# Low parts of branch weights made by VectorE a step earlier, twelve more blocks per layer moved from accumulating DMA to VectorE, and the vector transposes asked for later

## The chip, the cores and the metric

The kernel runs on one core of one Trainium2 chip. The metric is the device time of one execution, in microseconds (us). "Before" is the kernel without the change, "after" the kernel with it.

## What is computed

The reference is a two-layer encoder over two sequences of 256 positions, 1024 channels wide, in float32. Each layer normalises its input, multiplies it by one wide matrix, feeds five branches from the columns of the product (differential attention, a short gated convolution, a Conformer convolution of 31 taps, latent attention, attention to a memory), multiplies each branch by its own 512x1024 matrix, mixes the five by sigmoid gates and projects the mixture once more:

```python
h = _rms_norm(x, norm_pre)
proj = h @ w_in
(a_q, a_k, a_v, a_z, b_b, b_c, b_x, b_z, c_glu, c_z,
 d_cq, d_ckv, d_kr, d_z, e_q, e_z, gates) = jnp.split(proj, split_idx, axis=-1)
...
u = _dwconv(glu_a * jax.nn.sigmoid(glu_b), conf_dw_w) + conf_dw_b
o_c = jax.nn.silu(_layer_norm(u, conf_ln_g, conf_ln_b))
...
g = jax.nn.sigmoid(gates.reshape(B, S, N_BRANCHES, D_MODEL))
y = g[:, :, 0] * (outs[0] @ w_branch[0])
for i in range(1, N_BRANCHES):
    y = y + g[:, :, i] * (outs[i] @ w_branch[i])
y = y @ w_out
return x + _rms_norm(y, norm_post)
```

## The kernel before

Both sequences together are 512 rows. **Each product is made of three**: an operand x is kept as a high part (x rounded to TensorE's shorter float32 form) and a low part (x minus the high part), and `mm3` (L128 to L131) multiplies high by high (L129), high by low (L130 or L131) and low by high into one PSUM bank. So every weight block, 128 partitions by up to 1024 columns, is loaded by the SP queue into a tile of the `f` pool (12 buffers) and then split.

**Splitting** is `split` (L298 to L328). The high part `wh` is always a copy by ScalarE (L134). The low part `wl` is made in one of two ways: by VectorE, which subtracts (L295), or, where the block is marked `by_dma`, by ScalarE writing the negated block into `wl` (L322) and a DMA on GpSimd's queue that adds the block to it there (L323). `wh` and `wl` come from rings of NSPLIT = 4 buffers each, so the fifth split waits until the matmuls of the first are through. Marked in before are per layer the 36 blocks of the steps `s_q`, `s_k`, `zE`, `s_v`, `s_d` (832 columns wide), `bsteps[0]` and `bsteps[1]`, and the 20 blocks `wb` of the branch matrices: 112 in all.

**The order of the work** is a list of steps. A full step is 24 matmuls of 512 columns. Per layer it runs through value, key and memory products, the Conformer's gate product (`cglu`), `s_q`, `s_k`, `zE`, `s_v`, `s_d`, `bsteps[0]`, two small steps of the latent attention, `bsteps[1]`, `zC`, `zA`, `zD`, then five gate branches and the output product. A gate branch is seven products of gates (the last are called S4 and X22; X22 reads the two blocks `V4`) and four `b_step`s, which multiply the branch by its blocks `wb` 0 to 3: two steps on `wb` 0 and 1, then two on `wb` 2 and 3. Attention, layer norms and the 31 taps of the convolution (L622, L626) are background work, `bg`, of which a piece is written out after each step. Taps are tied by `issue_after` to the last VectorE subtraction written out ahead of them.

**When a block is split** is set by `issue_splits` (L1233), called ahead of each step: it splits on to the fourth block counted from the step's own first. Two blocks `o` per branch (the branch's activations) have room of their own outside the rings but are counted here, too. At X22's step the four are `V4` 0 and 1 and `o` 0 and 1, so all four `wb` are split at the first `b_step`.

**At the start** the small parameter vectors are loaded into rows of one buffer, `vecs`. `setup_vectors` transposes them on TensorE (L203) into `chv` and makes the lambda of the differential attention; it is called ahead of the first step.

Of the kernel before, what the change touches and what calls it, by code (L numbers as in the profile page):

```python
# [41 lines left out]
NSPLIT = 4  # L42
# [36 lines left out]
def body(ctx, tc, xp, xs_, mp, ms, norm_pre, w_in, diff_lambda, diff_subln, sconv_w,  # L79
# [23 lines left out]
    def nm(s):  # L103
        uid[0] += 1
        return f"{s}_{uid[0]}"
# [7 lines left out]
    def f4(dt=F32):  # L113
        return wk.tile([128, D], dt, tag="f4", name=nm("f4"), bufs=12)

    def m2(dt=F32):
        return wk.tile([128, 512], dt, tag="m2", name=nm("m2"), bufs=10)
# [7 lines left out]
    def att(slot, shape=None, dt=F32):  # L125
        return big.tile(shape or [128, 4, 512], dt, tag=f"att{slot}", name=nm(f"att{slot}"))
# [54 lines left out]
        nc.gpsimd.dma_start(dl, diff_lambda.rearrange("l a d -> (l a d)").partition_broadcast(128))  # L181
        yield

    vecs = att(8)
    rowsm, rows1, rows5, dl = vecs[:, 0, 0:128], vecs[:, 1, 0:128], vecs[:, 2], vecs[:, 3]

    def setup_mem_gains():
        t1 = trb()
# [11 lines left out]
    def setup_vectors():  # L200
        t5 = trb()
        for m in range(4):
            nc.tensor.transpose(t5[:, m * NR5:(m + 1) * NR5], rows5[0:NR5, m * 128:(m + 1) * 128],  # L203
                                ident[0:NR5, 0:NR5])
        copy(chv, t5[:, 0:4 * NR5].rearrange("p (m r) -> p m r", m=4))
        d4 = dl.rearrange("p (l a b d) -> p l a b d", l=DEPTH, a=2, b=2)
        pr = m2()
        p4 = pr[:, 0:DEPTH * 128].rearrange("p (l a d) -> p l a d", l=DEPTH, a=2)
        for li in range(DEPTH):
            nc.vector.tensor_mul(p4[:, li], d4[:, li, :, 0], d4[:, li, :, 1])  # L210
        s4 = sm(4, "lam")
        nc.vector.tensor_reduce(s4, p4.rearrange("p l a d -> p (l a) d"), AX.X, ALU.add)
        e4 = sm(4, "lam")
        nc.scalar.activation(e4, s4, AF.Exp)
        e2 = e4.rearrange("p (l a) -> p l a", a=2)
        nc.vector.tensor_sub(nlam.rearrange("p (l o) -> p l o", o=1), e2[:, :, 1:2], e2[:, :, 0:1])
        for li in range(DEPTH):
            nc.vector.tensor_scalar(nlam[:, li:li + 1], nlam[:, li:li + 1], -LAM_INIT[li], None, ALU.add)
# [113 lines left out]
    bg = []  # L332
# [201 lines left out]
    def layer(li):  # L534
# [51 lines left out]
        s_q = b_steps(wi, OFF["a_q"], 512, hT, post_qk("qT", 0))  # L586
        s_k = b_steps(wi, OFF["a_k"], 512, hT, post_qk("kT", 1))
# [9 lines left out]
        s_v = b_steps(wi, OFF["a_v"], 512, hT, post_va)  # L597
# [115 lines left out]
        zE = z_out(4, OFF["e_z"], "oE", 4)  # L713
# [33 lines left out]
        bsteps = []  # L747
# [42 lines left out]
        s_d = b_steps(wi, OFF["d_c"], 416, hT, post_d)  # L790
# [63 lines left out]
                              for s in range(2) for h0 in (0, 2)], 2))  # L854
        s_mq, s_mkv = Step(pq, pe_mq, post_mq), Step(pkv, pe_mkv, post_mkv)

        for s_ in s_q + s_k + zE + s_v + s_d + bsteps[0] + bsteps[1]:
            for pc in s_.pieces:
                pc.raw.by_dma = True
        steps.extend(cglu + s_q + s_k + zE + s_v + s_d + bsteps[0] + [s_mq, s_mkv] + bsteps[1] + zC + zA + zD)  # L860
# [95 lines left out]
        def gate_branch(n):  # L956
            i, q = ORDER[n], qs4[n]
            nxt = early(qs4[n + 1]) if n + 1 < NB else None
            item = {}
# [40 lines left out]
                add("o", lambda j=j: ozt[j], j, L_(4 + j), dest=o_room(j))  # L1000
            for j in range(4):
                add("wb", (lambda j=j: wbt[j]), j, L_(6, 7) if j == 0 else [], after=A_(2 + j) if j < 2 else None)
                item["wb", j].by_dma = True

            def product(x, w, bank, first, last):

# [200 lines left out]
    raws = []  # L1207
    for s_ in steps:
        for pc in s_.pieces:
            if pc.raw not in raws:  # L1210
                raws.append(pc.raw)
        s_.base = min((raws.index(pc.raw) for pc in s_.pieces), default=len(raws))
    loads = []
    for raw in raws:
        loads.extend(raw.loads)
        raw.need = len(loads)
    nl, nsp = [0], [0]

    def issue_raws(most=1 << 30):
# [11 lines left out]
        issue_raws()  # L1231

    def issue_splits(s_):  # L1233
        while nsp[0] < min(len(raws), s_.base + NSPLIT):
            split_next()

    def run():
# [56 lines left out]
            some_consts(99)  # L1294
        st["memT"] = (hs, ls)
        setup_gains()
        setup_vectors()

        def first_x():
            hs = [big.tile([128, 4, 512], F32R, tag=f"hTh{g}", name=nm("hTh")) for g in range(2)]  # L1300
# [19 lines left out]
        bg_drain()  # L1320

    run()


# [42 lines left out]
```

## Time and profile before

| | |
|---|---|
| time, median of 3 runs | 1652.76 us (1647.35 to 1655.71) |
| the profiled execution | 1652.49 us, of which the span from first to last instruction is 1650.7 us |
| TensorE (PE) busy | 1608.2 us, 97% of the span |
| VectorE (DVE) | 1104.1 us, 67% |
| ScalarE (ACT) | 924.0 us, 56% |
| GpSimd (POOL) | 179.9 us, 11% |
| mean granted TensorE clock | 0.997 |

TensorE is busy nearly always, so what matters are the few stretches in which it stands still and the few in which its clock is granted at half. The profile names for every wait what ended it. A busy share is of the whole span; the stages differ, and one of them may have VectorE full while another leaves it idle.

### The profile page before, as it was taken

The page shows a single profiled execution, that of the slowest core. Times are in us where ns is not written, and L with a number is a line of the kernel's source. Part 1 is how long each engine was busy: PE and PEld are TensorE (multiplying, and loading weights), DVE is VectorE, ACT ScalarE, POOL GpSimd, SP SyncE. Part 2 cuts the span into 40 slices and gives each one's busy share as a digit, 9 for nine tenths or more (in the row PEclk, how much of TensorE's full clock was granted, in tenths as well). Part 3 has the DMA queues.
Part 4 walks back from the last instruction along what each step waited for, and adds up shares of the span by engine and source line. Part 5 has one row for each costly group of instructions (what it writes and reads, how often), then busy time and mean ns, then how long its engine had stood idle before and what let it go on. Part 6 is the DMA issues. An engine that isn't in the chain of part 4 may idle for free.

```text
span 1650.7 us, 20815 instructions
## 1 busy us (share of the span) xinstructions
PE 1608.2 (97%) x7658; PEld 1333.3 (81%) x7658; DVE 1104.1 (67%) x1788; ACT 924.0 (56%) x1562; POOL 179.9 (11%) x248
## 2 busy tenths in 40 slices
PE   6999999999999999999999999999999999999998
PEld 5888887778888888787888888877888877877886
DVE  5459935778884675674672799268779755865753
ACT  5446547798444744645453655577964545545542
POOL 3001122111000000001020011221100000000010
PEclk9999999999999999999999999999999999999999
DMA  8317866545536546546461297665455357357341
GB/s 284 101 37 190 209 157 137 128 115 153 172 122 178 153 131 175 159 135 167 151 188 30 71 231 176 142 139 131 115 162 185 117 142 204 107 159 196 103 115 51
DMA packets 137350, 240.25 MB, mean 146 GB/s; under 512 B 15455, under 2 KB 67717, under 8 KB 137248
## 3 DMA queue, kind: packets, MB, share of 16 engines
q1 hardware_dynamic: 114176, 159.40, 31.3%
q0 software_dynamic: 22464, 78.46, 22.0%
q8 instruction: 60, 0.98, 0.2%
q10 hardware_dynamic: 608, 1.06, 0.2%
q14 instruction: 42, 0.34, 0.1%
HBM read 166.27 MB, written 14.68 MB: 110 GB/s over the span
## 4 chain that ended last, share of the span: by engine, by line
PE 38%; issue 7%; DMA 3%; DVE 3%; ACT 2%; POOL 0%; POOLq 0%; DVEq 0%; ACTq 0%
PE acc L130 11%; PE acc L129 11%; PE acc L131 11%; DMA wl<-f 1%; DMA f<-in_w_in_dram 1%; DVE wl L295 1%; PE tr L431 1%; ACT wh L134 1%; PE tr L239 0%; ACT att L134 0%; PE tr L1088 0%; PE tr L513 0%; PE tr L129 0%; PE tr L131 0%; PE tr L130 0%
## 5 line engine op out<-in xcount | busy, mean ns | idle before, releaser
L134 ACT ACTIVATE wh<-f 128x1024 fp32r<-128x1024 f32 (+1 forms) x276 | 288.7, 1051 | 259.1 <-PE acc L130 100.3
L295 DVE TENSOR_TENSOR wl<-f,wh 128x1024 fp32r<-128x1024 f32 (+1 forms) x164 | 199.6, 1219 | 131.6 <-ACT wh L134 128.4
L129 PE MATMUL acc<-hTh,wh 128*128 128x512 f32 x704 | 276.8, 393 | 0.0
L130 PE MATMUL acc<-hTl,wh 128*128 128x512 f32 x704 | 275.6, 391 | 0.0
L131 PE MATMUL acc<-hTh,wl 128*128 128x512 f32 x704 | 275.0, 391 | 0.0
L323 POOL DMA_DIRECT2D wl<-f x112 | 97.7, 872 | 890.2 <-ACT wl L322 864.5
L129 PE MATMUL acc<-wh,hTh 128*128 128x512 f32 (+1 forms) x496 | 191.5, 386 | 0.3 <-DVE m L701 0.3
L131 PE MATMUL acc<-wh,hTl 128*128 128x512 f32 (+1 forms) x496 | 190.6, 384 | 0.0
L130 PE MATMUL acc<-wl,hTh 128*128 128x512 f32 (+1 forms) x496 | 190.6, 384 | 0.0
L130 PE MATMUL acc<-wl,att 128*128 128x512 f32 x392 | 156.8, 400 | 13.2 <-DMA wl<-f 12.2
L626 DVE SCALAR_TENSOR_TENSOR att<-att,chv,att 128x496 f32<-128x496 f32 (+13 forms) x240 | 164.6, 736 | 0.7
L322 ACT ACTIVATE wl<-f 128x1024 fp32r<-128x1024 f32 (+1 forms) x112 | 116.8, 1043 | 76.6 <-PE acc L130 76.6
L129 PE MATMUL acc<-wh,att 128*128 128x512 f32 x392 | 156.2, 399 | 1.8 <-ACT att L134 1.7
L131 PE MATMUL acc<-wh,att 128*128 128x512 f32 x392 | 154.6, 395 | 0.0
L129 PEld LDWEIGHTS acc<-hTh,wh 128*128 128x128 f32 x704 | 132.3, 188 | 27.2
L131 PEld LDWEIGHTS acc<-hTh,wl 128*128 128x128 f32 x704 | 132.2, 188 | 27.3
L130 PEld LDWEIGHTS acc<-hTl,wh 128*128 128x128 f32 x704 | 132.3, 188 | 25.7
L134 ACT ACTIVATE wh<-att 128x1024 fp32r<-128x1024 f32 x60 | 63.2, 1056 | 111.6 <-PE acc L131 104.0
L129 PE MATMUL acc<-wh,S 128*128 128x512 f32 x320 | 124.5, 389 | 0.0
L130 PE MATMUL acc<-wl,S 128*128 128x512 f32 x320 | 124.5, 389 | 0.0
L131 PE MATMUL acc<-wh,S 128*128 128x512 f32 x320 | 124.5, 389 | 0.0
L129 PEld LDWEIGHTS acc<-wh,hTh 128*128 128x128 f32 x496 | 93.1, 188 | 17.7 <-DVE m L701 0.8
(212 smaller groups left out, 2837.0 us busy)
## 6 DMA issues: line engine op xcount, KB each, us to landing
f<-in_w_in_dram SPq DMA_DIRECT2D x172, 512.0 KB, 4.2
wl<-f POOLq DMA_DIRECT2D x104, 512.0 KB, 5.3
f<-in_w_branch_dram SPq DMA_DIRECT2D x40, 512.0 KB, 4.9
oz<-m POOLq DMA_DIRECT2D x40, 256.0 KB, 2.9
att<-in_w_in_dram SPq DMA_DIRECT2D x20, 512.0 KB, 4.5
f<-oz SPq DMA_DIRECT2D x20, 512.0 KB, 3.5
f<-in_mem_w_kv_dram SPq DMA_DIRECT2D x16, 512.0 KB, 6.6
f<-in_w_out_dram SPq DMA_DIRECT2D x16, 512.0 KB, 4.2
```

What stands on the lines that cost most here:

```text
L129: nc.tensor.matmul(out, ah, bh, start=first, stop=False, **kw)
L130: nc.tensor.matmul(out, ah, bl, start=False, stop=False, **kw)
L131: nc.tensor.matmul(out, al, bh, start=False, stop=last, **kw)
L134: nc.scalar.activation(out, in_, AF.Copy)
L295: return nc.vector.tensor_sub(lo, src, hi.bitcast(F32)).ins
L322: nc.scalar.activation(raw.lo, src, AF.Copy, scale=-1.0)
L323: nc.gpsimd.dma_start(raw.lo, src, accum_op=ALU.add)
L431: nc.tensor.transpose(tr[:, k * S + q * 128:k * S + q * 128 + 128], ps[q][:, k * 128:(k + 1) * 128], ident)
L626: nc.vector.scalar_tensor_tensor(av[:, :, lo:hi], uv[:, :, lo + d:hi + d], w, av[:, :, lo:hi], ALU.mult, ALU.add)
```

## The change

There are three edits.

1. `issue_splits` counts ring buffers instead of blocks, and blocks with room of their own are split as soon as they come up. The two `o` of a branch go one step earlier, and `wb` 0 and 1 are split at X22's step; `wb` 2 and 3 stay at the first `b_step`.
2. `wb` 0 and 1 of each branch (10 blocks per layer) are no longer marked `by_dma`, nor are the 4 blocks of `s_d` and the 8 of `bsteps[1]`: 44 blocks over both layers lose an instruction on ScalarE (L322) and a DMA on GpSimd's queue (L323) and get a subtraction on VectorE (L295). 68 blocks stay with the DMA.
3. `setup_vectors` is called from the background work, after the sixth step instead of ahead of the first, and `vecs` lies in two smaller buffers that it can hold for longer.

```diff
@@ -181,8 +181,8 @@
         nc.gpsimd.dma_start(dl, diff_lambda.rearrange("l a d -> (l a d)").partition_broadcast(128))
         yield
 
-    vecs = att(8)
-    rowsm, rows1, rows5, dl = vecs[:, 0, 0:128], vecs[:, 1, 0:128], vecs[:, 2], vecs[:, 3]
+    vecs, vec5 = m2(), f4()
+    rowsm, rows1, rows5, dl = vecs[:, 0:128], vecs[:, 128:256], vec5[:, 0:512], vec5[:, 512:1024]
 
     def setup_mem_gains():
         t1 = trb()
@@ -854,7 +854,7 @@
                               for s in range(2) for h0 in (0, 2)], 2))
         s_mq, s_mkv = Step(pq, pe_mq, post_mq), Step(pkv, pe_mkv, post_mkv)
 
-        for s_ in s_q + s_k + zE + s_v + s_d + bsteps[0] + bsteps[1]:
+        for s_ in s_q + s_k + zE + s_v + bsteps[0]:
             for pc in s_.pieces:
                 pc.raw.by_dma = True
         steps.extend(cglu + s_q + s_k + zE + s_v + s_d + bsteps[0] + [s_mq, s_mkv] + bsteps[1] + zC + zA + zD)
@@ -1000,7 +1000,7 @@
                 add("o", lambda j=j: ozt[j], j, L_(4 + j), dest=o_room(j))
             for j in range(4):
                 add("wb", (lambda j=j: wbt[j]), j, L_(6, 7) if j == 0 else [], after=A_(2 + j) if j < 2 else None)
-                item["wb", j].by_dma = True
+                item["wb", j].by_dma = j >= 2
 
             def product(x, w, bank, first, last):
 
@@ -1209,11 +1209,14 @@
         for pc in s_.pieces:
             if pc.raw not in raws:
                 raws.append(pc.raw)
-        s_.base = min((raws.index(pc.raw) for pc in s_.pieces), default=len(raws))
+        s_.raws = [raws.index(pc.raw) for pc in s_.pieces]
     loads = []
+    ring = 0
     for raw in raws:
         loads.extend(raw.loads)
         raw.need = len(loads)
+        raw.ring = ring
+        ring += raw.dest is None
     nl, nsp = [0], [0]
 
     def issue_raws(most=1 << 30):
@@ -1231,7 +1234,8 @@
         issue_raws()
 
     def issue_splits(s_):
-        while nsp[0] < min(len(raws), s_.base + NSPLIT):
+        base = min((raws[i].ring for i in s_.raws), default=ring)
+        while nsp[0] < len(raws) and (raws[nsp[0]].dest is not None or raws[nsp[0]].ring < base + NSPLIT):
             split_next()
 
     def run():
@@ -1294,7 +1298,12 @@
             some_consts(99)
         st["memT"] = (hs, ls)
         setup_gains()
-        setup_vectors()
+
+        def vectors():
+            for _ in range(5):
+                yield
+            setup_vectors()
+        bg.append(vectors())
 
         def first_x():
             hs = [big.tile([128, 4, 512], F32R, tag=f"hTh{g}", name=nm("hTh")) for g in range(2)]
```

The order of instructions on each engine shows it at three places. In the rows, `wl` and `wh` are the parts of a weight block, `m` and `acc` a gate and its bank, numbers those of buffers.

**First place: the end of a gate branch's products (layer 0, first branch).** ScalarE in before; the four `wl` by L322 are those of `wb` 0 to 3:

```order
L1033 ACTIVATE m_852_4725<-acc_4491 128x512
L322 ACTIVATE wl_4768<-f_783_4326 128x1024
L134 ACTIVATE wh_4767<-f_783_4326 128x1024
L1033 ACTIVATE m_853_4726<-acc_4492 128x512
L134 ACTIVATE wh_4777<-f_805_4481 128x1024
L322 ACTIVATE wl_4778<-f_805_4481 128x1024
L1028 ACTIVATE m_828_4601<-m_828_4601 128x512
L322 ACTIVATE wl_4784<-f_806_4483 128x1024
L134 ACTIVATE wh_4783<-f_806_4483 128x1024
L134 ACTIVATE wh_4788<-f_807_4485 128x1024
L1028 ACTIVATE m_829_4602<-m_829_4602 128x512
L322 ACTIVATE wl_4789<-f_807_4485 128x1024
```

ScalarE in after:

```order
L1033 ACTIVATE m_857_4724<-acc_4480 128x512
L134 ACTIVATE wh_4728<-f_784_4315 128x1024
L1033 ACTIVATE m_858_4725<-acc_4481 128x512
L134 ACTIVATE wh_4737<-f_806_4470 128x1024
L1028 ACTIVATE m_829_4590<-m_829_4590 128x512
L322 ACTIVATE wl_4771<-f_807_4472 128x1024
L134 ACTIVATE wh_4770<-f_807_4472 128x1024
L134 ACTIVATE wh_4775<-f_808_4474 128x1024
L1028 ACTIVATE m_830_4591<-m_830_4591 128x512
L322 ACTIVATE wl_4776<-f_808_4474 128x1024
```

The copies `wh` of `wb` 0 and 1 stand where the first L322 stood, and the two L322 that are left are those of `wb` 2 and 3. VectorE there in before:

```order
L1026 TENSOR_TENSOR m_835_4640<-m_835_4640,acc_4656 128x512
L295 TENSOR_TENSOR wl_4687<-att_772_4247,wh_4686 128x1024
L1026 TENSOR_TENSOR m_836_4641<-m_836_4641,acc_4657 128x512
L295 TENSOR_TENSOR wl_4695<-att_772_4247,wh_4694 128x1024
L1026 TENSOR_TENSOR m_828_4601<-m_828_4601,acc_4656 128x512
L1026 TENSOR_TENSOR m_829_4602<-m_829_4602,acc_4657 128x512
L1068 TENSOR_TENSOR att_870_4819<-acc_4793,m_812_4517 128x512
```

VectorE in after, from the same merge (L1026) on:

```order
L1026 TENSOR_TENSOR m_836_4629<-m_836_4629,acc_4645 128x512
L295 TENSOR_TENSOR wl_4676<-att_773_4236,wh_4675 128x1024
L1026 TENSOR_TENSOR m_837_4630<-m_837_4630,acc_4646 128x512
L295 TENSOR_TENSOR wl_4684<-att_773_4236,wh_4683 128x1024
L295 TENSOR_TENSOR wl_4729<-f_784_4315,wh_4728 128x1024
L295 TENSOR_TENSOR wl_4738<-f_806_4470,wh_4737 128x1024
L1026 TENSOR_TENSOR m_829_4590<-m_829_4590,acc_4645 128x512
L1026 TENSOR_TENSOR m_830_4591<-m_830_4591,acc_4646 128x512
L1068 TENSOR_TENSOR att_871_4806<-acc_4780,m_813_4506 128x512
```

The two subtractions of `wb` 0 and 1 have come in behind those of `V4` and ahead of X22's merge.

**Second place: VectorE from the last steps of `zE` and `s_v` to the first attention step under `s_d` (layer 0).** Before, the convolution's taps (L626) run ahead and the maximum of the scores (L406) follows the gates (L701, L707):

```order
L626 SCALAR_TENSOR_TENSOR att_182_926<-att_181_925,chv,att_182_926 128x2x248
L626 SCALAR_TENSOR_TENSOR att_182_926<-att_181_925,chv,att_182_926 128x2x247
L701 TENSOR_TENSOR m_331_1914<-acc_1889,m_331_1914 128x512
L707 TENSOR_TENSOR m_331_1914<-m_331_1914,att_155_782 128x512
L406 TENSOR_REDUCE mx_2172<-sc_2159 128x4
L408 TENSOR_SCALAR nmx_2174<-mx_2172 128x4
L415 RECIPROCAL rc_2182<-su_2177 128x4
```

After, the four subtractions of `s_d` stand there, and the taps that stood ahead of the gates now stand among and behind the subtractions:

```order
L295 TENSOR_TENSOR wl_2039<-f_335_1929,wh_2038 128x832
L626 SCALAR_TENSOR_TENSOR att_183_927<-att_182_926,chv,att_183_927 128x2x255
L626 SCALAR_TENSOR_TENSOR att_183_927<-att_182_926,chv,att_183_927 128x2x254
L626 SCALAR_TENSOR_TENSOR att_183_927<-att_182_926,chv,att_183_927 128x2x253
L626 SCALAR_TENSOR_TENSOR att_183_927<-att_182_926,chv,att_183_927 128x2x252
L295 TENSOR_TENSOR wl_2079<-f_338_1936,wh_2078 128x832
L626 SCALAR_TENSOR_TENSOR att_183_927<-att_182_926,chv,att_183_927 128x2x251
L622 TENSOR_SCALAR att_183_927<-att_182_926,chv 128x512
```

and on to the maximum:

```order
L626 SCALAR_TENSOR_TENSOR att_183_927<-att_182_926,chv,att_183_927 128x2x244
L626 SCALAR_TENSOR_TENSOR att_183_927<-att_182_926,chv,att_183_927 128x2x246
L626 SCALAR_TENSOR_TENSOR att_183_927<-att_182_926,chv,att_183_927 128x2x245 x2
L406 TENSOR_REDUCE mx_2169<-sc_2156 128x4
L626 SCALAR_TENSOR_TENSOR att_183_927<-att_182_926,chv,att_183_927 128x2x244
L408 TENSOR_SCALAR nmx_2171<-mx_2169 128x4
L626 SCALAR_TENSOR_TENSOR att_183_927<-att_182_926,chv,att_183_927 128x2x246
L626 SCALAR_TENSOR_TENSOR att_183_927<-att_182_926,chv,att_183_927 128x2x243
```

Eight of the `bsteps[1]` subtractions come in likewise some hundred rows later.

**Third place: the vector transposes on TensorE.** Before, among the first memory products:

```order
L131 MATMUL acc_299<-wh_227,att_15_107 128x512
L129 MATMUL acc_299<-wh_259,att_13_105 128x512
L203 MATMUL tr_283<-ident,att_1_88 128x74 x4
L130 MATMUL acc_299<-wl_260,att_13_105 128x512
L131 MATMUL acc_299<-wh_259,att_15_107 128x512
L131 MATMUL acc_302<-wh_168,att_14_106 128x512
```

After, L203 stands 154 rows later, between two steps:

```order
L130 MATMUL acc_612<-att_16_108,wh_444 128x512
L131 MATMUL acc_612<-att_14_106,wl_445 128x512
L203 MATMUL tr_638<-ident,f_2_89 128x74 x4
L129 MATMUL acc_666<-hTh_336,wh_555 128x512
L130 MATMUL acc_666<-hTl_338,wh_555 128x512
```

Elsewhere TensorE's order is nearly the same, and that of the SP queue is unchanged.

## Rows read from the trace of the kernel before

**Rows 1.** The page, part 1: busy time, share of the span, instructions.

```profile
PE 1608.2 (97%) x7658; PEld 1333.3 (81%) x7658; DVE 1104.1 (67%) x1788; ACT 924.0 (56%) x1562; POOL 179.9 (11%) x248
```

**Rows 2.** TensorE's waits: total us, times, longest us.

```profile
PE acc L130 <- DMA wl<-f: 12.2, 11, 2.0
PE tr L129 <- ACT att L134: 4.5, 2, 2.2
...
PE tr L467 <- ACT att L134: 1.2, 2, 0.6
```

**Rows 3.** Line 323, the accumulating DMA: durations in ns, and its landing.

```profile
L323 POOL DMA_DIRECT2D wl<-f x112: 843/862/1008, 129.8 to 1578.0; - x112
...
DMA to landing us min/median/max: 3.9/5.2/9.0
```

**Rows 4.** TensorE's timeline, gate branch, layer 1: start, us, operation, [idle before].

```profile
1325.88 0.39 PE L129 MATMUL acc<-wh,att 128*128 128x512 f32 x1
...
1327.24 0.39 PE L129 MATMUL acc<-wh,att 128*128 128x512 f32 x1
1329.65 0.50 PE L130 MATMUL acc<-wl,att 128*128 128x512 f32 x1 [2.02 <-DMA wl<-f]
```

**Rows 5.** GpSimd's timeline in the same branch: the DMAs of wb 1 and wb 3.

```profile
1324.04 0.87 POOL L323 DMA_DIRECT2D wl<-f  x1 [2.73 <-ACT wl L322]
...
1329.32 0.85 POOL L323 DMA_DIRECT2D wl<-f  x1 [2.50 <-ACT wl L322]
```

**Rows 6.** ScalarE's timeline in the same branch, the first splits of wb.

```profile
1319.05 1.06 ACT L322 ACTIVATE wl<-f 128x1024 fp32r<-128x1024 f32 x1 [0.54 <-PE acc L130]
...
1322.39 1.05 ACT L322 ACTIVATE wl<-f 128x1024 fp32r<-128x1024 f32 x1
```

**Rows 7.** VectorE's timeline: X22's merge in the same branch.

```profile
1323.36 0.69 DVE L1026 TENSOR_TENSOR m<-m,acc 128x512 f32<-128x512 f32 x1 [5.46 <-PE acc L131]
```

**Rows 8.** Groups by line and shape: busy us, mean ns | idle before.

```profile
L295 DVE TENSOR_TENSOR wl<-f,wh 128x1024 fp32r<-128x1024 f32 x162 | 197.7, 1223 | 129.0 <-ACT wh L134 125.8 <-PE tr L431 3.0
...
L322 ACT ACTIVATE wl<-f 128x1024 fp32r<-128x1024 f32 x104 | 109.6, 1054 | 54.0 <-PE acc L130 54.0
...
L626 DVE SCALAR_TENSOR_TENSOR att<-att,chv,att 128x506 f32<-128x506 f32 x16 | 12.0, 750 | 0.1
```

**Rows 9.** Windows: busy us of PE, PEld, DVE, ACT, POOL; PE clock; DMA share, GB/s.

```profile
33.20:36.50 3.30, 3.30 (x9) 2.54 (x8) 2.34 (x5) 1.69 (x3) 0.55 (x1) 0.50 0.00 0
1036.00:1064.00 28.00, 28.00 (x141) 24.44 (x140) 0.00 (x0) 12.05 (x16) 4.84 (x6) 1.00 0.70 146
1064.00:1220.00 156.00, 151.02 (x820) 124.65 (x821) 115.25 (x284) 127.48 (x308) 26.91 (x35) 1.00 0.55 132
1140.00:1160.00 20.00, 18.96 (x100) 14.19 (x99) 18.20 (x44) 18.92 (x47) 4.91 (x7) 1.00 0.52 131
1330.20:1333.60 3.40, 3.40 (x10) 2.61 (x9) 0.69 (x1) 0.00 (x0) 0.00 (x0) 0.51 1.04 239
```

**Rows 10.** TensorE's timeline near the start.

```profile
31.90 0.45 PE L203 MATMUL tr<-ident,att 74*128 74x74 f32 x4 [2.62 <-DMA att<-in_diff_lambda_dram]
```

**Rows 11.** VectorE's timeline in the same place.

```profile
28.77 1.38 DVE L231 TENSOR_TENSOR att<-m,att 128x512 fp32r<-128x512 f32 x2
```

**Rows 12.** ScalarE's timeline, layer 1: the last low part of s_d, before.

```profile
1053.84 0.90 ACT L322 ACTIVATE wl<-f 128x832 fp32r<-128x832 f32 x1 [0.53 <-PE acc L130]
```

**Rows 13.** VectorE's timeline under s_d and bsteps[0], layer 1: two softmax maxima.

```profile
1064.00 1.23 DVE L406 TENSOR_REDUCE mx<-sc 128x4 f32<-128x1024 f32 x1 [28.29 <-PE sc L446]
...
1080.84 0.17 DVE L408 TENSOR_SCALAR nmx<-mx 128x4 f32<-128x4 f32 x1
```

**Rows 14.** TensorE's longest wait behind them, layer 1.

```profile
1085.21 0.38 PE L129 MATMUL tr<-f,m 128*128 128x256 f32 x1 [2.24 <-ACT att L134]
```

**Rows 15.** A small GpSimd operation while VectorE subtracts.

```profile
849.36 1.47 POOL L140 TENSOR_TENSOR r<-e,mhalf 128x1 f32<-128x1 f32 x1 [1.54 <-DVE e L138]
```

**Rows 16.** VectorE at that moment.

```profile
849.18 1.23 DVE L295 TENSOR_TENSOR wl<-f,wh 128x1024 fp32r<-128x1024 f32 x1
```

## The prediction

> **What bounds the kernel now.** The page comes first. TensorE is busy 1608.2 us of a span of 1650.7 us, 97% [rows 1], so no shortening of another engine's work can bring more than the 42.5 us in which TensorE stands still, plus what a half clock takes. The next view is TensorE's waits by what ended them. The largest entry is 12.2 us in 11 waits for the accumulating DMA of a low part, each of at most 2.0 us [rows 2]. By TensorE's timeline all eleven stand in the first `b_step` of a gate branch (ten branches, one of them with two such waits), and one of them is shown with its surroundings: the step begins at 1325.88, its seventh matmul at 1327.24, and the eighth, which needs the low part of `wb` 1 (some of the others are stopped by `wb` 0), starts only at 1329.65, after 2.02 us [rows 4]. The DMA of that part was issued at 1324.04 [rows 5], and such a DMA lands 5.2 us after its issue in the median, 9.0 us at worst [rows 3]. So the wait is the DMA's own length, begun too late: ScalarE writes its negated copy at 1322.39 [rows 6], for a product that begins 3.5 us later.
>
> After that wait the granted clock is 0.51 for the 3.4 us from 1330.20 to 1333.60 (the lower level, 1.2 of 2.4 GHz), against 1.00 in the rows of the stages around it [rows 9]. A half clock for 3.4 us loses 3.4 x 0.5 = 1.7 us. The same stands near the start: a wait of 2.62 us for the load of the lambda, in front of the transposes L203 [rows 10], and then 3.3 us at 0.50 [rows 9]. TensorE's wait of 2.24 us at 1085.21 [rows 14] is followed by none: the stage from 1064 to 1220 has 1.00 [rows 9]. An idle time of some 2 us may thus be followed by a slow stretch or not.
>
> **The gate branches.** The change splits `wb` 0 and 1 at X22's step and by VectorE. The first copy `wh` takes the place of the L322 at 1319.05, and such a ScalarE instruction takes 1.05 us [rows 6, 8], so it is through at about 1320.1; the subtraction takes 1.22 us [rows 8] and ends at 1321.4. The second copy is the third or fourth ScalarE instruction there, where L322 of 1322.39 was the fifth; it ends by 1322.5, its subtraction by 1323.7. `wb` 1 is needed at 1329.65 - 2.02 = 1327.63, so 3.9 us are left. Is VectorE free? Ahead of X22's merge it is idle for 5.46 us, to 1323.36 [rows 7], and 2.44 us of subtraction go into that; if the second ends at 1323.7 the merge is 0.35 us late, and what hangs on the merge are sigmoids and gates, not a matmul. `wb` 2 and 3 stay with the DMA and now stand behind a product that is no longer held up. The last DMA is issued at 1329.32 [rows 5] and lands at 1334.5, by the worst landing at 1338.3 [rows 3]. Matmuls follow each other at (1327.24 - 1325.88) / 6 = 0.227 us [rows 4]; the low part of `wb` 3 is used 48 matmuls behind that of `wb` 1, so at 1327.47 + 10.9 = 1338.4. Even the slowest landing is then in time, by 0.1 us. I take all of **-12.2 us**, and **-1.7 us** for the slow stretch. Bound from the other side: if `wb` 2 or 3 comes late in half of the branches, half is left, -6.
>
> **The start.** With L203 asked for 154 instructions later, its load has long landed when its turn comes. TensorE goes on 2.62 us earlier [rows 10]; what it needs next from VectorE are the low parts of L231, written by 30.15 [rows 11], so at least 31.90 - 30.15 = 1.75 us are gained if these stop it at once, 2.62 if not. I take **-2.6 us** and, for the slow stretch that followed, **-1.7 us** (bound: 0). In its new place L203 costs the same matmuls. `chv`, which it makes, is wanted first by the short convolution and the taps, behind `cglu`.
>
> **The removed DMAs of `s_d` and `bsteps[1]`.** None of the eleven waits stands there, so removing them gains nothing at TensorE. The 44 L322 give ScalarE back 44 x 1.05 = 46 us [rows 8], the 44 issues give GpSimd 38 us at 0.86 [rows 3]. TensorE does wait for ScalarE's copies in the attention, 4.5 us in two layers [rows 2], so a gain of up to 0.5 us a layer can't be excluded; I take none.
>
> **The added subtractions of `s_d` and `bsteps[1]`.** Per layer these are 4 x 1.22 x 832/1024 + 8 x 1.22 = 13.7 us more for VectorE, and they hold back taps: being tied to the last subtraction, those that ran ahead of the gates of `zE` come after `s_d`'s subtractions. Before, VectorE is idle for 28.29 us, until the first maximum L406 at 1064.00 [rows 13], and not busy at all in 1036 to 1064 [rows 9]. After, the last subtraction of `s_d` follows a copy that can begin when L322 did, at 1053.84 [rows 12], so it ends at about 1053.84 + 0.9 + 1.0 = 1055.7. 13 taps stand between it and L406 in the new order. One takes 0.75 us by its own row and near 0.69 in a row of them, the overlap counted once (an estimate), so they end at 1055.7 + 9.0 = 1064.7: the maximum is 0.7 us late. The second maximum now stands behind all the rope and norm work of `s_d` instead of in the middle of it. Adding the durations in that order brings its L408 from 1080.84 [rows 13] to 1083.2, 2.3 us late (an estimate). TensorE's wait at 1085.21 [rows 14] hangs on that chain; between them lie the exponential and the normalisation, which can close up, and I let 1.0 us come through. The next wait of that chain, 0.6 us in each layer [rows 2], then falls away: net **+0.4 us** a layer, bounds -0.5 and +3 (the whole 2.3, and the first 0.7). In `bsteps[1]` two subtractions come between the layer norms and the maxima at a time. From 1140 to 1160 VectorE has 18.20 us of 20 full [rows 9], so there everything behind moves by about 2 us. Most of what moves is the Conformer's norm, whose transposes also stand later in TensorE's order: **+0.5 us** a layer, bounds 0 and +1.5. TensorE's longest wait rises from 2.24 to some 3.2 us in each layer, and an idle time of that size may bring a slow stretch of 1.7 us: I count one of the two, **+1.7 us**, bounds 0 and 3.4.
>
> A rule speaks against this part. While VectorE runs an operation with two inputs in SBUF, GpSimd may be held up: at 849.36 a power of one column takes 1.47 us [rows 15] beside a subtraction that runs from 849.18 [rows 16]. The Trainium skill, page "SBUF — State Buffer", section "Who interferes with whom", says that the two share a port pair under an exclusive lock; the trace agrees. By that rule, each of the two or three powers of the norms in `bsteps[1]` could be held by one subtraction, up to 1.2 us, which would make +0.5 there about +2. The DMA issues hardly show it: 843 to 1008 ns over 112 [rows 3].
>
> **The sum.** The profiled execution took 1652.49 us, 0.27 below the median of 1652.76. 1652.49 - 12.2 - 1.7 - 2.6 - 1.7 + 2 x 0.4 + 2 x 0.5 + 1.7 = 1637.8. I forecast **1638 us**, -0.9%. With all the bounds on the good side it would be 1652.5 - 18.2 - 1.0 = 1633; the likeliest case's own range is 1632 to 1644. The runs of before are spread by 1647 to 1656, so a difference within 0.5% (1644.5 to 1661) can hardly be told from none.
>
> **Rivals.** (1) *VectorE is too full under `s_d` and `bsteps[1]`.* For it: 13.7 us of subtractions and some 15 us of taps come to a stage of 156 us in which VectorE has 40.75 us idle [rows 9], in pieces. If the maxima hold TensorE up for another 5 to 7 us in each layer, 1637.8 + 2 x 5 to 1637.8 + 2 x 7 is 1648 to 1652. Against: 28 us of idle time lie just ahead. (2) *The gate branches keep half of their waits*, since `wb` 2 and 3 land late, or the copies of `wb` 0 wait for a ring buffer: 1637.8 + 6 + 1.7 = 1645. Against: 3.9 us of margin. (3) *Slower than before.* VectorE bounds the layer from `s_d` to the end of `bsteps[1]`: the maxima and normalisations come so late that TensorE has no other matmuls left to do meanwhile. The gains together are 18.2 us, so this decides from 18.2 / 2 = 9 us of extra waiting a layer. The 9.8 us of the eight subtractions of `bsteps[1]`, all on TensorE's path, and the 3 us of the upper bound under `s_d` make 12.8, and a slow stretch in each layer 1.7 more: 1652.5 - 18.2 + 2 x 14.5 = 1663. For it speaks 1140 to 1160, where VectorE is nearly full [rows 9]; against it the stages on both sides, where it is not. (4) *The order on paper isn't the time's*: the subtractions wait in VectorE's queue for copies that come late, and `wb` is ready no sooner: 1652.5 - 4.3 + 3 = 1651.
>
> **Chances.** The forecast 0.62, rival 1 0.15, rival 2 0.12, rival 3 0.07, rival 4 0.04. Faster by over 0.5%: nearly all of the first, half of the second rival, and the fifth of the first in which it comes smaller: 0.71. Slower: 0.07 and little more, 0.08. Within: 0.21. For 8 in 10 the range takes in rival 2 and the lower part of rival 1: 1631 to 1649.
>
> **What would show it.** Right: no wait for the low parts of `wb` in the first `b_step`s; L203 without a wait and a clock of 1.00 from 33 to 37 us; the maximum after `s_d` at most 1 us later against its step, and TensorE's wait behind it at 3 to 3.5 us. Wrong: waits for `wl` by L295 at TensorE in `b_step`s (rival 2 or 4); idle time of TensorE from `s_d` to `bsteps[1]` above 10 us per layer, where it is now 156 - 151.02 = 5.0 us [rows 9] (rivals 1 and 3); new stretches at half clock.

## The result and the profile after

The kernel after took **1629.9 us** in the median of 4 runs (1629.67 to 1630.96), against 1652.08 (1647.35 to 1655.71) before: ratio 0.9869, 95% interval 0.9843 to 0.9894. A second comparison of the same two kernels gave 1629.74 against 1650.39, ratio 0.9877 (0.9862 to 0.9892). The forecast was 1638, with a range from 1631 to 1649: the sign was right, the gain was about half as large again as forecast, and the time lies 1 us below the range.

The page of after, span and part 1; it answers to [rows 1]:

```profile
span 1628.0 us, 20690 instructions
...
PE 1600.2 (98%) x7658; PEld 1332.7 (82%) x7658; DVE 1153.1 (71%) x1832; ACT 889.9 (55%) x1522; POOL 145.3 (9%) x204
```

The instruction counts are those of the edit: 44 more on VectorE, 44 fewer on GpSimd, and on ScalarE 44 times L322 less and four table loads more. VectorE has 49 us more to do and TensorE stands still for 27.8 us instead of 42.5. TensorE's waits in after (line, what it waited for: total us, times, longest), to be held against [rows 2]:

```profile
PE tr L129 <- ACT att L134: 5.0, 2, 2.5
...
PE tr L467 <- ACT att L134: 1.2, 2, 0.7
PE acc L130 <- DVE wl L295: 0.9, 2, 0.5
PE tr L1088 <- DVE yTl L231: 0.7, 1, 0.7
PE tr L513 <- DVE m L654: 0.6, 2, 0.3
```

The entry of 12.2 us for the accumulating DMA is gone and nothing has come in its place: the two waits of 0.9 us in all for a low part from VectorE stand in the first 20 us of the kernel. The wait in front of L203 is gone, too.

**Where the time went** can be read from matmuls that stand at the same place of the program in both kernels: both traces hold 7658 of them, and each of the nine below has the same number in both. TensorE's timeline of before, at nine such places (start, us, operation):

```profile
104.60 0.40 PE L129 MATMUL acc<-hTh,wh 128*128 128x512 f32 x1
...
242.40 0.35 PE L129 MATMUL acc<-wh,hTh 128*128 128x416 f32 x1
...
288.43 0.40 PE L129 MATMUL acc<-hTh,wh 128*128 128x512 f32 x1
...
350.56 0.48 PE L129 MATMUL acc<-hTh,wh 128*128 128x512 f32 x1
...
427.39 0.40 PE L129 MATMUL acc<-hTh,wh 128*128 128x512 f32 x1
...
916.73 0.40 PE L129 MATMUL acc<-hTh,wh 128*128 128x512 f32 x1
...
1099.85 0.40 PE L129 MATMUL acc<-hTh,wh 128*128 128x512 f32 x1
...
1161.98 0.48 PE L129 MATMUL acc<-hTh,wh 128*128 128x512 f32 x1
...
1238.80 0.40 PE L129 MATMUL acc<-hTh,wh 128*128 128x512 f32 x1
```

The same matmuls in after:

```profile
100.60 0.40 PE L129 MATMUL acc<-hTh,wh 128*128 128x512 f32 x1
...
237.63 0.35 PE L129 MATMUL acc<-wh,hTh 128*128 128x416 f32 x1
...
285.08 0.40 PE L129 MATMUL acc<-hTh,wh 128*128 128x512 f32 x1
...
346.62 0.48 PE L129 MATMUL acc<-hTh,wh 128*128 128x512 f32 x1
...
423.51 0.40 PE L129 MATMUL acc<-hTh,wh 128*128 128x512 f32 x1
...
904.80 0.40 PE L129 MATMUL acc<-hTh,wh 128*128 128x512 f32 x1
...
1087.97 0.40 PE L129 MATMUL acc<-hTh,wh 128*128 128x512 f32 x1
...
1149.47 0.48 PE L129 MATMUL acc<-hTh,wh 128*128 128x512 f32 x1
...
1226.35 0.40 PE L129 MATMUL acc<-hTh,wh 128*128 128x512 f32 x1
```

The differences make a ledger. After is ahead by 4.00 us at the first place, then 4.77, 3.35, 3.94, 3.88, 11.93, 11.88, 12.51 and 12.45, and by 1650.7 - 1628.0 = 22.7 at the end. By stage:

| stage | forecast, us | gained in the trace, us |
|---|---|---|
| start, to the first attention | 4.3 | 4.0 |
| layer 0, up to the head of `s_d` | 0 | 0.8 |
| layer 0, `s_d` and `bsteps[0]` | -0.4 and one slow stretch of -1.7 | -1.4, one slow stretch in it |
| layer 0, `bsteps[1]` | -0.5 | 0.6 |
| layer 0, gate branches and what lies up to layer 1's attention | 5.8 | 8.05 |
| layer 1, `s_d` and `bsteps[0]` | -0.4 | -0.05 |
| layer 1, `bsteps[1]` | -0.5 | 0.6 |
| layer 1, gate branches to the end | 6.4 + 1.7 | 10.2 |

(The waits of [rows 2] fall 5.8 to 6.4 on the two layers.) So the gate branches gave 18.3 us where 13.9 were forecast, and the new subtractions cost nothing in sum where 3.5 were forecast. Read at the first matmul of each first `b_step` and 24 matmuls later, the ledger puts 17.8 us into these ten steps. Some 0.6 came at TensorE's wait at L1088, which was 1.28 us in before and is 0.72 in after.

**The gate branch** shown in [rows 4 to 7], in after. ScalarE (start, us, operation):

```profile
1306.86 1.06 ACT L134 ACTIVATE wh<-f 128x1024 fp32r<-128x1024 f32 x1 [0.81 <-PE acc L131]
...
1308.67 1.05 ACT L134 ACTIVATE wh<-f 128x1024 fp32r<-128x1024 f32 x1
```

VectorE:

```profile
1307.95 1.23 DVE L295 TENSOR_TENSOR wl<-f,wh 128x1024 fp32r<-128x1024 f32 x1 [2.52 <-ACT wh L134]
1309.75 1.23 DVE L295 TENSOR_TENSOR wl<-f,wh 128x1024 fp32r<-128x1024 f32 x1 [0.57 <-ACT wh L134]
```

TensorE, the first and the eighth matmul of the first `b_step`:

```profile
1313.41 0.39 PE L129 MATMUL acc<-wh,att 128*128 128x512 f32 x1
...
1315.00 0.39 PE L130 MATMUL acc<-wl,att 128*128 128x512 f32 x1
```

The second low part is ready at 1310.98 and used at 1315.00: 4.0 us of margin, where 3.9 were forecast.

**Why the gates gave more than their waits.** A plain wait of before, in layer 0, where no slow stretch follows:

```profile
576.92 0.39 PE L129 MATMUL acc<-wh,att 128*128 128x512 f32 x1
578.85 0.50 PE L130 MATMUL acc<-wl,att 128*128 128x512 f32 x1 [1.54 <-DMA wl<-f]
579.19 0.40 PE L131 MATMUL acc<-wh,att 128*128 128x512 f32 x1
```

Without a wait these matmuls start every 0.227 us. From the first to the second it is 1.93, 1.70 too long, and from the second to the third 0.34, 0.11 too long: 1.81 us were lost where the profile lists 1.54. The list counts idle time from the modelled end of the matmul before, 0.39 us behind its start, by which time a successor would already have run for 0.16 us; and the first matmul after a stop lets the next one follow only 0.34 us behind it. That is 0.27 us for each listed wait, 3.0 us for eleven. Counted in this way over all matmuls of 512 columns, the ten gate branches of before lost 17.2 us (1.7 of it in the slow stretch), and those of after nowhere more than 0.1 us at one place.

**What the added subtractions did.** VectorE in after, layer 1, the two maxima of [rows 13]:

```profile
1052.56 1.22 DVE L406 TENSOR_REDUCE mx<-sc 128x4 f32<-128x1024 f32 x1
...
1070.91 0.16 DVE L408 TENSOR_SCALAR nmx<-mx 128x4 f32<-128x4 f32 x1
```

TensorE is 11.93 us ahead there, so the first maximum is 1052.56 - (1064.00 - 11.93) = 0.5 us late (forecast 0.7), and the second scale 1070.91 - (1080.84 - 11.93) = 2.0 us late (forecast 2.3). But TensorE's wait behind them, which answers to [rows 14], is hardly longer:

```profile
1071.25 0.39 PE L130 MATMUL acc<-hTl,wh 128*128 128x512 f32 x1
1074.11 0.39 PE L129 MATMUL tr<-f,m 128*128 128x256 f32 x1 [2.48 <-ACT att L134]
```

It is 2.48 us, 0.24 more than before. In after, 35 matmuls of 512 columns stand in the run ahead of the waiting product, in before 31 (counted in the two traces): four more, 0.9 us of work, cover part of the lateness.

Of the 0.8 us gained ahead of `s_d` in layer 0, 0.6 stand at one matmul of `zE`. In before six taps run on VectorE ahead of a gate (L701), and TensorE waits for that gate:

```profile
219.30 4.61 DVE L626 SCALAR_TENSOR_TENSOR att<-att,chv,att 128x504 f32<-128x504 f32 x6
223.82 0.68 DVE L701 TENSOR_TENSOR m<-acc,m 128x512 f32<-128x512 f32 x1
```

```profile
224.56 0.50 PE L129 MATMUL acc<-wh,hTh 128*128 128x512 f32 x1 [0.34 <-DVE m L701]
```

In after these taps stand among and behind `s_d`'s subtractions, and this wait is gone.

### The profile page after: what moved, and what is told of

The parts are those of the page before. It is cut to its first block, busy times and chain, and to the rows that moved or that the text cites. A ratio compares the mean times of both kernels' runs of the same rounds, so it can differ in the third digit from the quotient of the medians.

```text
span 1628.0 us, 20690 instructions
## 1 busy us (share of the span) xinstructions
PE 1600.2 (98%) x7658; PEld 1332.7 (82%) x7658; DVE 1153.1 (71%) x1832; ACT 889.9 (55%) x1522; POOL 145.3 (9%) x204
## 4 chain that ended last, share of the span: by engine, by line
PE 48%; DVE 3%; ACT 1%; issue 1%; POOL 0%; POOLq 0%; DVEq 0%; ACTq 0%
PE acc L129 15%; PE acc L130 15%; PE acc L131 15%; DVE att L626 1%; PE tr L431 1%; PE tr L239 0%; ACT wh L134 0%; PE tr L1088 0%; PE tr L513 0%; PE tr L131 0%; PE tr L130 0%; PE tr L129 0%; PE sc L130 0%; PE sc L131 0%; PE sc L129 0%
## 5 line engine op out<-in xcount | busy, mean ns | idle before, releaser
L295 DVE TENSOR_TENSOR wl<-f,wh 128x1024 fp32r<-128x1024 f32 (+1 forms) x208 | 251.7, 1212 | 176.7 <-ACT wh L134 173.6
L626 DVE SCALAR_TENSOR_TENSOR att<-att,chv,att 128x502 f32<-128x502 f32 (+13 forms) x240 | 166.7, 730 | 1.3
L131 PEld LDWEIGHTS acc<-hTh,wl 128*128 128x128 f32 x704 | 132.5, 188 | 27.8
L130 PE MATMUL acc<-wl,att 128*128 128x512 f32 x392 | 153.4, 392 | 1.2 <-DVE wl L295 0.9
L323 POOL DMA_DIRECT2D wl<-f x68 | 59.3, 872 | 853.1 <-ACT wl L322 828.0
L131 PEld LDWEIGHTS acc<-wh,hTl 128*128 128x128 f32 x496 | 93.1, 188 | 17.1
```

The source lines that it names most:

```text
L130: nc.tensor.matmul(out, ah, bl, start=False, stop=False, **kw)
L131: nc.tensor.matmul(out, al, bh, start=False, stop=last, **kw)
L295: return nc.vector.tensor_sub(lo, src, hi.bitcast(F32)).ins
L323: nc.gpsimd.dma_start(raw.lo, src, accum_op=ALU.add)
L626: nc.vector.scalar_tensor_tensor(av[:, :, lo:hi], uv[:, :, lo + d:hi + d], w, av[:, :, lo:hi], ALU.mult, ALU.add)
```

## Experiments

"Listed waits" are those for the accumulating DMA in gate branches. A slow stretch is some 3.4 us in which the granted clock is 0.50 and matmuls of 512 columns start every 0.43 us instead of 0.23, counted from 30 us on. Both are of the profiled execution, the times medians.

| kernel | time, us | ratio to before (95%) | listed waits | slow stretches |
|---|---|---|---|---|
| before | 1650.0 to 1652.1 in the four comparisons | 1 | 11, 12.2 us | 2 |
| after | 1629.9 | 0.9869 (0.9843 to 0.9894) | none | 1 |
| branch blocks, both edits | 1633.96 | 0.9899 (0.9879 to 0.9919) | none | 1 |
| count only | 1650.7 | 1.0002 (0.9992 to 1.0011) | 12, 11.5 us | 4 |
| VectorE for branch blocks only | 1635.43 | 0.9907 (0.9892 to 0.9922) | none | 1 |
| vectors only | 1649.46 | 0.9992 (0.9981 to 1.0003) | 12, 11.6 us | 1 |
| `s_d`, `bsteps[1]` only | 1649.3 | 0.9991 (0.9981 to 1.0001) | 12, 11.8 us | 3 |
| after, `s_d` by DMA | 1629.08 | 0.9867 (0.9848 to 0.9887) | none | 0 |
| after, `bsteps[1]` by DMA | 1630.87 | 0.9877 (0.9860 to 0.9893) | none | 1 |
| after again | 1629.74 | 0.9877 (0.9862 to 0.9892) | none | 1 |
| after without the count | 1629.93 | 0.9877 (0.9860 to 0.9893) | none | 1 |
| after, later product | 1627.3 | 0.9864 (0.9849 to 0.9879) | none | 1, of 6.8 us |

**The branch blocks alone.** Before, with these two edits of the change:

```diff
-        while nsp[0] < min(len(raws), s_.base + NSPLIT):
+        base = min((raws[i].ring for i in s_.raws), default=ring)
+        while nsp[0] < len(raws) and (raws[nsp[0]].dest is not None or raws[nsp[0]].ring < base + NSPLIT):
...
-                item["wb", j].by_dma = True
+                item["wb", j].by_dma = j >= 2
```

> The kernel before with the count of ring buffers and VectorE's subtractions for the first two branch blocks only; the other two edits are left out. Theory: each of the eleven listed waits costs about 0.27 us more than the idle time listed for it, so the gate branches gain 11 x 0.27 + 12.2 + 1.7 for the slow stretch = 16.9 us, and 0.6 us at the output product: ratio 0.989, and nothing before the gates changes by more than 0.3 us. Rival: the gates give only the 13.9 us of waits and slow stretch that the forecast counted, and the rest of what after gained there comes from the other edits, through fewer DMAs in flight: ratio 0.9915.

Measured: 0.9899, which is 16.5 us; the theory's 0.989 lies in the interval, and the rival's 0.9915 too, so the time alone doesn't part them. The trace does: by the same ledger the gate branches gain 8.2 and 10.25 us, as much as between before and after, without the other edits. The extra gain belongs to these edits. The theory's other half, that nothing ahead of the gates moves by more than 0.3 us, did not come: the start is 2.1 us ahead of before's, and a slow stretch in layer 1 costs 1.55.

**The count alone**, that is the first part of that diff:

> The kernel before with the count of ring buffers only; the low parts of all four branch blocks are still made by ScalarE and the DMA. Theory: the split was already placed as early as a ring buffer is free, and being asked for a step earlier moves it by less than 1 us; 8 to 11 of the waits stay and the time is within 4 us of before. Rival: asking earlier is what removes the waits, and most of the 18 us of the gate branches come: ratio 0.990.

Measured 1.0002. The waits stay, in the first `b_step`s, twelve where the theory had 8 to 11; TensorE's list in this kernel:

```profile
PE acc L130 <- DMA wl<-f: 11.5, 12, 1.8
```

The traces show more than the time. This kernel and before hold the same 20815 instructions, and every engine runs its own in the same order. The new count leaves the program as it was: nothing is split a step earlier. So this run is before a second time, and its four slow stretches against two, and its L203 wait of 1.52 us against 2.62, are what one program differs by from one profiled execution to another.

**VectorE for the branch blocks without the count**, the second part of that diff:

> The kernel before with VectorE's subtractions for the first two branch blocks, without the count of ring buffers. Theory: the DMA's length was the wait, so this alone takes away all eleven waits: ratio 0.989, the same as with both. Rival: without the earlier split the copy comes too late, and waits of 0.5 to 1.5 us stay, now for VectorE: ratio 0.994 or more.

Measured 0.9907, no such wait, and the gates gain 8.3 and 10.3 us by the ledger. The rival falls. The reason stands in the order of the instructions: the copy and the subtraction of `wb` 0 and 1 already follow those of `V4` here, ahead of X22's merge. This kernel, too, holds the same instructions in the same order as the one with both edits, so the 1.5 us between their medians (1635.43 and 1633.96) are not the count's. Of the change's first two edits the second did everything; "a step ahead" is a name. That a split's place is set by the ring buffer that it needs, and not by the step that asks for it, would explain this; it is argued, no run tests it.

**The vectors alone:**

```diff
-    vecs = att(8)
+    vecs, vec5 = m2(), f4()
...
-        setup_vectors()
+        bg.append(vectors())
```

> The kernel before with the vector transposes asked for later, alone. Theory: 4.0 us by the first 60 us (the wait of 2.62 us and the slow stretch behind it, as between before and after) and nothing later: ratio 0.9976. Rival: the slow stretch at the start comes anyway, and 2.3 us are left: ratio 0.9986.

Measured 0.9992 (0.9981 to 1.0003), 1.3 us; the theory's 0.9976 lies outside, the rival's 0.9986 inside. In this kernel's own trace no wait and no slow stretch come at L203, yet the first place of the ledger is 1.7 us ahead of before, not 4.0: its first matmul starts at 4.44 us instead of 3.81, and its clock rises to the upper level at 21.8 us instead of 16.1. The traces of the other kernels show that the profiled execution of before was no typical one, either. L203 in four kernels that keep its early place, first the branch blocks with both edits:

```profile
31.40 0.45 PE L203 MATMUL tr<-ident,att 74*128 74x74 f32 x4 [0.29 <-DVE att L231]
```

count only:

```profile
31.09 0.45 PE L203 MATMUL tr<-ident,att 74*128 74x74 f32 x4 [1.52 <-DMA att<-in_conf_ln_b_dram]
```

VectorE for branch blocks only:

```profile
31.58 0.45 PE L203 MATMUL tr<-ident,att 74*128 74x74 f32 x4 [1.41 <-DMA att<-in_conf_ln_b_dram]
```

`s_d` and `bsteps[1]` only:

```profile
31.64 0.45 PE L203 MATMUL tr<-ident,att 74*128 74x74 f32 x4 [2.19 <-DMA att<-in_diff_lambda_dram]
```

With the 2.62 of [rows 10] these are 0.3 to 2.6 us for the same instruction, and a slow stretch followed two of the five. The profiled execution of before was one of the dear ones. At the ledger's first place the five kernels with the early L203 are 0 to 2.4 us ahead of before (mean 1.3), the seven with the late one 1.7 to 4.0 (mean 3.0); the difference of 1.7 us fits the measured 1.3.

**The steps alone:**

```diff
-        for s_ in s_q + s_k + zE + s_v + s_d + bsteps[0] + bsteps[1]:
+        for s_ in s_q + s_k + zE + s_v + bsteps[0]:
```

> The kernel before with VectorE's subtractions for the 4 blocks of s_d and the 8 of bsteps[1] per layer, alone. Theory: as between the traces of before and after, up to 0.8 us gained at zE in the first layer, 0.2 us (1.4 with a slow stretch) lost under s_d and bsteps[0], 0.65 us gained in bsteps[1] of each layer: together a gain of 0 to 2 us, ratio 0.9988 to 1.000. Rival, as forecast: 0.9 us lost in each layer and a slow stretch: ratio 1.0015 to 1.002.

Measured 0.9991 (0.9981 to 1.0001): no loss; the rival's 1.0015 is excluded. By the ledger 0.7 us come at `zE` of layer 0 and 0.65 in `bsteps[1]` of each layer, and a slow stretch of about 1.5 follows TensorE's wait of 2.45 us in both layers, where the profile of before has none.

**After, with `s_d` by the DMA again:**

```diff
-        for s_ in s_q + s_k + zE + s_v + bsteps[0]:
+        for s_ in s_q + s_k + zE + s_v + s_d + bsteps[0]:
```

> The kernel after with the 4 blocks of s_d made by ScalarE and the DMA again. Theory: the taps run ahead of zE's gates again, so the 0.75 us of zE in the first layer are lost; the first softmax maximum is early again, TensorE's wait behind it falls from 2.48 to 2.24 us, and no slow stretch follows it: between 1 us faster and 1 us slower than after. Rival: the taps held back cost TensorE the 2.48 us wait: 2 to 4 us faster than after.

Measured 1629.08 against 1629.9 and 1629.74: no difference that the runs can tell. The wait is back at 2.21 us, the gain at `zE` falls from 0.8 to 0.2 us and that in `bsteps[1]` is there: as the theory had it. That no slow stretch follows its two waits proves nothing by itself, as the next but one run shows.

**After, with `bsteps[1]` by the DMA again**, the same line with `s_d` out and `bsteps[1]` in:

> The kernel after with the 8 blocks of bsteps[1] made by ScalarE and the DMA again. Theory: the later norms of the convolution let TensorE run its transposes in one piece, and that is worth 0.65 us a layer: 1 to 1.5 us slower than after. Rival: it is the taps and s_d that shift these transposes, and nothing changes in bsteps[1]: within 0.3 us of after by the trace.

Measured 1630.87 (1630.06 to 1631.39), 1.0 to 1.1 us above after. In its trace the gain at `zE` is there and that in `bsteps[1]` is gone. So the 0.65 us a layer come from the subtractions of `bsteps[1]`. The timeline shows what they do: in before the eight transposes L513 of the convolution's norm stand in two fours, between score matmuls, at 1153.03 and 1154.35; in after they stand as one run of eight at 1143.37, behind more products, and eleven of the twelve score matmuls (L446), too, are in one piece. TensorE's listed waits around them are no shorter (1.04 us in before from 1143.19 to 1160.92, 1.21 in the same part of after, from 1131.30 to 1148.40), so the gain lies outside the list. In that stretch TensorE changes between kinds of work 19 times in before and 17 times in after; that these changes cost the 0.65 us is argued, not shown.

**Chance or place?** The kernel after a second time:

> The kernel after, unchanged, a second time, to stand beside the next two on one chip. Theory: what is left of slow stretches is chance at TensorE's two waits of about 2.5 us, so the time is 1630 within 1.7 us, and each of the two waits may or may not be followed by one. Rival: the slow stretch of the first layer belongs to the kernel, and is there again, and none in the second layer.

In the first profile of after, the wait of 2.48 us in layer 0 is followed by a slow stretch and the equal wait in layer 1 is not. The window of that stretch (busy us of PE, PEld, DVE, ACT, POOL; PE clock; DMA share, GB/s):

```profile
271.40:274.80 3.40, 3.40 (x9) 2.67 (x8) 3.33 (x8) 2.65 (x5) 0.42 (x1) 0.50 0.00 0
```

In the second profile it is the other way round:

```profile
1074.90:1078.30 3.40, 3.40 (x9) 2.66 (x9) 3.33 (x8) 2.67 (x5) 0.41 (x1) 0.52 0.00 0
271.00:275.00 4.00, 4.00 (x24) 3.42 (x24) 3.96 (x10) 3.93 (x8) 0.00 (x0) 1.00 0.00 0
```

So the place isn't fixed. Over the eleven profiled executions that have these two waits of 2.2 to 2.5 us, 11 of the 22 waits were followed by a slow stretch. The rise of the clock at the start varies, too: it comes at 15.4 us in the first profile of after, whose first matmul starts at 3.6, and at 16.6 in the second, whose first matmul starts at 4.3. (Of that rise the Trainium skill, page "TensorE: Matmul & The Clock Gate", section "What's actually happening", says that it varies from run to run of the same kernel; these two traces agree. That a fall behind a wait varies is shown here by the traces alone.)

**After without the count:**

> The kernel after without the count of ring buffers. Theory: that edit alone moved nothing, and VectorE's subtractions stand early enough without it: within 1.5 us of after, no wait for low parts in the gate branches. Rival: it is needed once VectorE makes the parts of s_d and bsteps[1] too: waits of 0.5 us or more in some branches.

Measured 1629.93 against 1629.74 for after on the same chip, no such waits. Here, too, the trace holds the same instructions as after, 20690, in the same order on every engine: the count does nothing.

**After, with the product one step later.** The two waits of 2.48 us are the largest that are left behind the start, so the product that waits is asked for later:

```diff
         v = vals(va, s, h)
         yield
+        yield
         po = trb()
```

> The kernel after with the product of probabilities and values of the differential attention asked for one step later. Theory: TensorE's two waits of 2.48 us are for a transpose bank that ScalarE empties late; with more matmuls ahead of the waiting product they go, with 0.3 us each and the slow stretch of one of them: 4 to 7 us faster than after, 1623 to 1626. Rival: the wait moves to the next user of a bank, or the attention ends later and the gates' steps wait for it: between 2 us faster and 4 us slower than after.

Measured 1627.3 (1626.73 to 1629.04), against 1629.74 (1629.12 to 1630.49) for after on the same chip: 2.4 us faster, and the fastest kernel here. It lies between theory and rival. TensorE's waits in it:

```profile
PE tr L129 <- ACT att L134: 3.3, 2, 1.6
PE acc L129 <- DVE att L832: 3.1, 4, 1.5
PE sc L446 <- DVE f L295: 1.7, 2, 0.8
```

The two waits fell from 5.0 to 3.3 us in all, and two others grew, that for L832 from 1.6 (in after it is listed at L831). Part of the wait moved. Its one slow stretch lasts 6.8 us, twice the usual, and begins while TensorE stands in the first of the two waits; `s_d` and `bsteps[0]` of layer 0 lose 3.15 us against before in this execution.

## Why the prediction was right or wrong

**The gate branches: right in mechanism, mis-sized.** That the wait is the DMA's own length, that VectorE has room for two subtractions there, that `wb` 2 and 3 by the DMA come in time, all stood as put: the margin was 4.0 us, and no wait is left. The step that failed took the listed idle time as the cost. The term of -13.9 us measured -18.3: 3.0 of the difference are the 0.27 us that each of eleven waits cost beyond its listing, 0.6 the wait at L1088, which was not in the sum, and the rest, some 0.8, are delays in the same steps that are too short for the list. It is the same step that put the edge of the range too high: its best case, 1633, let no wait cost more than listed. Of the 8.0 us between the sum, 1637.8, and the profiled 1629.8 the gates make 4.4, the added subtractions 3.9 and the start -0.3.

**The credit to the earlier split: wrong.** The prediction spoke of splitting "at X22's step and by VectorE" as one thing. Count only gave 1.0002, VectorE only 0.9907. The count changes no instruction, so the text on the change is wrong where it has `o` and `wb` 0 and 1 split a step earlier by it: with the second edit alone the splits stand where they stand in after.

**The added subtractions: wrong sign.** The walk through VectorE's order was good to 0.3 us at both maxima. What failed is the step from there to TensorE: "I let 1.0 us come through" measured 0.24 in the wait, and the norms' transposes coming later, counted as +0.5 us a layer, measured -0.65. Both go with TensorE's order, four matmuls more ahead of the wait and the transposes in one run; that the transposes stand later was seen, the rest of that order was not compared. The next wait of that chain, at L467, which was to fall away with 0.6 us a layer, stayed: 1.2 us in two layers before and after. The gain at `zE` of 0.75 us in layer 0, where taps no longer stand ahead of the gate that TensorE waited for, was not seen either.

**The slow stretches: sizes right, certainty wrong.** One new stretch after the waits of `s_d` was counted, and one came; with 11 of 22 such waits followed by one, one of two is the likeliest number, and that just one came here is luck. But the two that were counted as gains are events of one execution. Before scatters from 1647 to 1656 us and after from 1629.1 to 1631.0; the executions of before differ in how many of their waits of around 2 us are followed by a slow stretch and in how long L203 waits, and after has two such waits left and no wait at L203. Before and count only, the same program, had two and four stretches in executions of 1652.5 and 1654.8 us. That this makes the whole of the scatter is argued from the traces, not shown run by run.

**The start: right for the profiled pair (4.0 for 4.3), too large in general.** Alone, the edit is worth 1.3 us, with an interval from 3.1 down to a loss of 0.5. The load that L203 waited for was not the lambda, as the prediction put it: in before the lambda lands at 32.73 us, behind L203's start at 31.90. What it waited for is the last load of the rows that it transposes, `in_conf_ln_b`, which lands at 31.55: in all five kernels with the early place L203 starts 0.34 to 0.38 us behind that landing, whatever the profile names.

**The rule on the shared port** was right in kind. The powers of the norm in `bsteps[1]`, L649, in after (durations in ns: least, median, largest):

```profile
L649 POOL TENSOR_TENSOR r1c<-e1c,mhalf x8: 547/667/1808, 336.9 to 1148.1; 128x1 f32<-128x1 f32 x8
```

Two of eight were held to 1.8 us while VectorE subtracted (the largest before was 0.67). The Trainium skill's page "SBUF — State Buffer", section "Who interferes with whom", says that a VectorE instruction with two SBUF inputs contends with a GpSimd instruction that reads SBUF; the trace agrees. What hangs on these powers are the transposes L513. TensorE now waits 0.3 us a layer for them, so the +2 us that the rule was given did not come.

**The rivals.** None came. From `s_d` to the end of `bsteps[1]` TensorE stands still for 5.5 us of 156 in layer 1, against 5.0 before: 0.5 us more, not the 5 us and more a layer of rivals 1 and 3. No `b_step` waits.

## What to carry to other kernels

A listed wait can cost more than its listing, here 0.27 us more each time: hold the start of the matmul behind it against the usual spacing, and look whether a slow stretch follows. An operand that is made by an engine with room, in 1.2 us, was better here than one made by a queue in 5.2. Asking for it earlier in the program need not move it: compare the order of the instructions before crediting such an edit. Before a single profiled execution is summed up, ask which of its waits are the same in every execution.

## What was not expected of the hardware

The same wait of 2.48 us, at the same instruction, is or isn't followed by 3.4 us at half clock, 1.4 to 1.7 us of loss, about one time in two. And L203 waits for 0.29 to 2.62 us at the start, though it starts within 0.8 us in the five kernels with its early place (31.09 to 31.90 us), as the load that it needs lands (30.74 to 31.55). What differs more is when TensorE comes to it: at 29.27 us in before and at 31.12 in the branch blocks with both edits, whose clock rose at 21.6 us instead of 16.1.
